# The output projection's last block of columns and the LayerNorm behind it, in halves

## The chip, the cores and the metric

The kernel runs on one core of a Trainium2 chip. The metric is the device time of one execution in microseconds, as a median of several runs. TensorE (PE) multiplies, VectorE (DVE), ScalarE (ACT) and GpSimd (POOL) work element by element, SyncE (SP) issues nearly all DMAs. Each engine works through its own queue in order and waits at semaphores for the others.

## The reference

An encoder layer over 256 tokens of 1,024 channels, all in float32. A mixer of three branches (gated linear attention, a Fourier mixing, cross-attention) ends in an output projection; its result is added to the scaled input and normalised. The normalised tokens go to a router, which picks 4 of 32 experts for each token, and to the experts:

```
h = layer_norm(DN_ALPHA * h + mix, ln1_g, ln1_b)      # mix = merged @ w_out + b_out
logits = h @ w_router + b_router                      # 1,024 x 32
top_val, top_idx = top_k(logits, 4);  top_w = softmax(top_val)
for each expert e: out = swiglu(h[tok] @ w_gu[e] + b_gu[e]) @ w_down[e] + b_down[e]
h = layer_norm(DN_ALPHA * h + weighted sum of out, ln2_g, ln2_b)
```

## The kernel before

Tokens lie in two groups of 128 partitions, tau 0 and tau 1 (`hs[tau]`, the same tiles as `h1[tau]`, 128 x 1024). In the mixer every product of the projections is made from split operands: `mm3` issues three matmuls (lines 144 to 146) of high and low parts for one step of 128 channels. A program planner orders the mixer's instructions on each engine and sets all semaphore waits from what the instructions read and write; the code sets none by hand. Within a `manual_schedule` block the order of the listed engines is that of the code.

The output projection is `project_tok(A["w_out"][0], ...)`, called twice, for columns 0 to 511 (`u == 0`) and 512 to 1023 (`u == 1`). Each call keeps two PSUM tiles of 128 x 512, one for each tau, and runs eight steps over the channels. In the first call both taus take each step in turn. In the second (`last`), all eight steps of tau 0 come first; then a written order for VectorE and TensorE begins (`K.order`, ended after `place(1)` and its picks in `moe`), tau 0 is evacuated, tau 1 has its 24 matmuls, and tau 1 is evacuated.

Evacuation is `ev_o` (lines 764 to 772). It adds the PSUM tile to the residual in `hs[tau]` and takes `bn_stats` over the 512 columns. In the second call it goes on to the LayerNorm: `bn_aggr`, the reciprocal root (`Rstd`: an add on VectorE, a power on GpSimd, in `end()` three small steps on VectorE) and two passes over 1,024 columns (lines 771 and 772), the first of which doesn't need the root.

`moe` takes over on the same written order. TensorE: two filling products of the identity (`spin`, line 901), `turn(0)` (eight transposes of tau 0, four to a PSUM tile, each taking every eighth column of `h1`, with a copy by ScalarE behind each four, lines 863 and 864), more filling, `score(0)` (line 870, the router's product with `wr`, 128 x 8 x 32), six filling products, `turn(1)`, filling, four steps of `score(1)`, `place(0)`, the other four, and the choice and gather for the first two experts. A product on float32 operands shows as two matmuls in the trace. VectorE goes from tau 1's LayerNorm to `choose(0)`, `place(0)`, `choose(1)`, `place(1)`.

The experts run two at a time in 16 pairs. Their weights, in tiles of mostly 2 MB on SyncE's queue (lines 796 and 804), go through a ring of ten buffers of 16 KB a partition, six of which are filled before the mixer ends; the other four and three further tiles use memory that the mixer's tiles gave back. A buffer is filled again as soon as TensorE has used it.

`project_T` (line 334 and on) serves the other projections: it fills a PSUM tile of two blocks of 256 columns with 24 matmuls each and then evacuates it; for the queries and keys by line 449, one instruction for each block of 256 columns.

The router's weights are loaded in the middle of the mixer by line 501, among other small loads of SyncE's queue.

Of the kernel before, what the change touches and what calls it, by code (L numbers as in the profile page):

```python
# [10 lines left out]
F32 = mybir.dt.float32  # L11
# [3 lines left out]
ALU = mybir.AluOpType  # L15
# [3 lines left out]
D = 1024  # L19
# [121 lines left out]
def mm3(K, out, w, x, first, last):  # L141
    nc = K.nc
    (wh, wl), (xh, xl) = w, x
    nc.tensor.matmul(out, wh, xh, start=first, stop=False)  # L144
    nc.tensor.matmul(out, wh, xl, start=False, stop=False)  # L145
    nc.tensor.matmul(out, wl, xh, start=False, stop=last)  # L146
# [9 lines left out]
def split_w(K, w):  # L156

    m, n = w.shape[1:]
    parts = []
    for name in ("whi", "wlo"):  # L160
        t = K.wspl.tile([128, 1024], F32R, name=name, tag=name)[:, :m * n]
        parts.append(t.rearrange("p (m n) -> p m n", m=m))
    split(K, w, *parts)
    return parts
# [33 lines left out]
def mixer(ctx: ExitStack, K, A):  # L198
    tc, nc = K.tc, K.nc
# [14 lines left out]
    def late(ap, src):  # L214
        nc.sync.dma_start(ap, src)

    def load_bc(name, ap, tag):
        t = at(name, (D,), tag=tag)
        late(t, ap[None, :].broadcast_to([128, D]))
        return t  # L220

    w_in, b_in = A["w_in"][0], A["b_in"][0]
    hs = K.h1
# [24 lines left out]
    part = K.early.tile([128, 4, D], F32, name="parts", tag="ring2")  # L248
# [19 lines left out]
    with tc.manual_schedule(engines={mybir.EngineType.DVE, mybir.EngineType.PE, mybir.EngineType.Activation}):  # L268
# [9 lines left out]
        for tau, r in enumerate((r0, r1)):  # L278
            rs_[tau] = r.end()
            c = half[2]  # L280
            t = K.small.tile([128, 8], F32, name="nmr", tag="sm")[:, 0:1]
# [4 lines left out]
            c = half[0]  # L286
            V.scalar_tensor_tensor(hs[tau][:, c], xs[tau][:, c], mvs[tau][:, 0:1], g[:, c], ALU.subtract, ALU.mult)
        for tau in range(2):
            c = half[0]
            V.scalar_tensor_tensor(hs[tau][:, c], hs[tau][:, c], rs_[tau], b[:, c], ALU.mult, ALU.add)  # L290
        for tau in range(2):
            c = half[1]
# [36 lines left out]
    def project_tok(W, c0, X, evac, last=False):  # L329

        ws = []
        for h in range(2):
            w = K.wraw.tile([128, 2048], F32, name="wraw", tag="wraw").rearrange("p (k n) -> p k n", k=4)
            nc.sync.dma_start(w, W[h * 512:h * 512 + 512, c0:c0 + 512].rearrange("(k p) n -> p k n", p=128))
            ws.append(w)
        ps = [K.ps.tile([128, 512], F32, name="pj", tag="pj") for _ in range(2)]

        def run(tau, k, parts):
            hi, lo = parts
            mm3(K, ps[tau], X.at(k, slice(tau * 128, tau * 128 + 128)), (hi[:, k % 2], lo[:, k % 2]), k == 0, k == 7)  # L340
        allp = []
        for k in range(0, 8, 2):
            parts = split_w(K, ws[k // 4][:, k % 4:k % 4 + 2])
            allp.append(parts)
            for tau in range(1 if last else 2):
                for i in range(2):
                    run(tau, k + i, parts)
            bg.tick(K.TICK)
        if last:
            K.order = tc.manual_schedule(engines={mybir.EngineType.DVE, mybir.EngineType.PE})  # L350
            K.order.__enter__()
        evac(0, ps[0])
        if last:
            for k in range(8):
                run(1, k, allp[k // 2])
        evac(1, ps[1])


    ps = K.ps.tile([128, 2, S], F32, name="pj", tag="pj")
    hi, lo = wlr_parts  # L360
# [131 lines left out]
    for u in range(2):  # L492
        sl = slice(u * 512, (u + 1) * 512)
        project_tok(w_in, 1024 + u * 512, hT,
                    lambda tau, ps: nc.vector.tensor_tensor(v[tau][:, sl], ps, bv[:, sl], ALU.add))

    late(cm, A["c_mix"])
    late(K.kp[:, 128:], A["c_keep"][:, 128:])
    late(K.wr, A["w_router"][0].rearrange("(p k) e -> p k e", p=128))
    late(K.br, A["b_router"].broadcast_to([128, NE]))  # L500
    for n in range(4):
        late(K.bias[n * 32:n * 32 + 32, 0:512], A["b_gu"][0, :, n * 512:n * 512 + 512])
# [4 lines left out]
    g1, b1 = load_bc("g1", A["ln1_g"][0], tag="g"), load_bc("b1", A["ln1_b"][0], tag="g")  # L507
# [51 lines left out]

    mv = at("mv", (2, 512), tag="o")  # L560
    project_tok(A["w_mem_kv"][0], 512, mT, lambda tau, ps: nc.scalar.activation(mv[:, tau], ps, AF.Copy))
    fnT = at("fnT", tag="o")
    project_T(w_in, 3104, 4, hT, 8, ev_id(fnT, 24))
# [185 lines left out]
        project_T(A[name][0], 0, 8, X, kn, ev_y)  # L749


    st = [K.small.tile([128, 2, 6], F32, name=f"st{t}", tag="st") for t in range(2)]

    class Merged:
        @staticmethod
# [2 lines left out]
    for u in range(2):  # L758
        sl = slice(u * 512, (u + 1) * 512)

        if u == 0:
            K.early_load(4)

        def ev_o(tau, ps):
            nc.vector.tensor_tensor(hs[tau][:, sl], hs[tau][:, sl], ps, ALU.add)
            nc.vector.bn_stats(st[tau][:, u], hs[tau][:, sl])
            if u == 1:
                mv_ = K.small.tile([128, 2], F32, name="bmv", tag="mv")
                nc.vector.bn_aggr(mv_, st[tau])
                r = Rstd(K, mv_[:, 1:2], LN_EPS, 1)  # L770
                nc.vector.scalar_tensor_tensor(hs[tau], hs[tau], mv_[:, 0:1], g1, ALU.subtract, ALU.mult)
                nc.vector.scalar_tensor_tensor(hs[tau], hs[tau], r.end(), b1, ALU.mult, ALU.add)
        project_tok(A["w_out"][0], u * 512, Merged, ev_o, last=u == 1)


# [41 lines left out]
def moe(ctx, K, A):  # L817
    tc, nc = K.tc, K.nc
    h1 = K.h1
# [4 lines left out]
    ps = ctx.enter_context(tc.tile_pool(name="eps", bufs=2, space=PSUM, reuse_waits="tile"))  # L824
# [33 lines left out]
    def turn(tau):  # L858
        hrT[tau] = big.tile([128, 8, 128], F32, name="hrT", tag="xT")
        for j in range(2):  # L860
            t = yps().rearrange("p (c n) -> p c n", c=4)
            for c in range(4):
                nc.tensor.transpose(t[:, c], h1[tau][:, j * 4 + c::8], K.ident)
            nc.scalar.activation(hrT[tau][:, j * 4:j * 4 + 4], t, AF.Copy)

    def score(tau, ks):
# [37 lines left out]

    spin(2)
    turn(0)
    spin(2)
    score(0, slice(0, 8))
    spin(6)
    turn(1)  # L910
    spin(2)
    choose(0)
# [233 lines left out]
    def back(y, p, G):  # L1146
        for n in range(2):
            combine(y, G, slice(n * 512, n * 512 + 512), p == 0, (yps, mps)[n])

    with tc.manual_schedule(engines={mybir.EngineType.DVE, mybir.EngineType.PE, mybir.EngineType.Activation}):  # L1150
# [4 lines left out]
        for p in range(1, NE // 2):  # L1155
            first = []
            a0, a = a, up(p, xT, (lambda: first.append(after(0, a, P))) if p == 1 else None)
            if p == 1:
                held = first[0]
                t = K.res.tile([128, 4, D], F32, name="sum", tag="sum", bufs=1)  # L1160
# [16 lines left out]
        st = last_down(last, now[0], G, w, parts, lambda: back(y, last - 1, held[1]))  # L1177
# [117 lines left out]
def block(tc, A):  # L1295
# [4 lines left out]
    with tc.tile_pool(name="cst", bufs=1) as c, tc.tile_pool(name="small", bufs=8) as sm, \  # L1300
# [17 lines left out]
        def early_load(e):  # L1318
# [3 lines left out]
            K.slot_no += 1  # L1322
        K.early_load = early_load
        mixer(K, A)
        with tc.tile_pool(name="res", bufs=1, side="right", reuse_waits="tile") as c:
            K.wts = c.tile([128, 2, NE], F32, name="wts")
# [39 lines left out]
```

## Time and profile before

| | before |
|---|---|
| median of 3 runs | 1233.61 us (1233.05 to 1233.71) |
| profiled execution | 1233.55 us, span 1231.5 us |
| busy: TensorE, its weight loads | 1164.2 us (95%), 639.3 us (52%) |
| busy: VectorE, ScalarE, GpSimd | 381.3 us (31%), 260.0 us (21%), 47.8 us (4%) |
| DMA | 458.24 MB, mean 372 GB/s |

The span is divided by the mixer (to about 306 us), the router (to about 320 us) and the experts. Matmuls are pipelined and their ends are modelled. The granted clock is the share of TensorE's full clock: 1.00 is 2.4 GHz and 0.50 is 1.2 GHz.

### The profile page before, as it was taken

To read this page: it belongs to the slowest core of one execution; us is meant where nothing else is said; L and a number is where in the kernel's file an instruction comes from. 1 tells how busy PE (TensorE), PEld (TensorE's weight loads), DVE (VectorE), ACT (ScalarE), POOL (GpSimd) and SP (SyncE) were. 2 spreads that over 40 slices of the span, in tenths; PEclk is the share of its full clock that TensorE was granted. 3 is DMA by queue.
4 is the path that set the end of the run, shared out by engine and by line. 5 is a ranking of instruction groups with operands and counts; after the bars stand their busy time and mean duration, and the time that the engine had idled before them with its cause. 6 is when DMAs were issued, how large, how long until landed. Compare 5 with 4: busy or idle time off the path is not lost.

```text
span 1231.5 us, 14887 instructions
## 1 busy us (share of the span) xinstructions
PE 1164.2 (95%) x6413; PEld 639.3 (52%) x6413; DVE 381.3 (31%) x591; ACT 260.0 (21%) x453; POOL 47.8 (4%) x70
## 2 busy tenths in 40 slices
PE   6999999999999999999989898999898989899995
PEld 6898999998544343443334242434243424333333
DVE  7995465486211131111202030211111111111124
ACT  4775555453111010100101010201010101000010
POOL 2150000000000000000000000000000000000000
PEclk8999999999999999999999999999999999999998
DMA  8755557687999999999999999999999999999994
GB/s 284 254 195 171 193 191 245 254 310 273 384 412 411 395 430 432 428 431 430 430 432 429 431 431 431 431 429 431 431 428 434 429 429 433 429 430 431 427 422 161
DMA packets 77241, 458.24 MB, mean 372 GB/s; under 512 B 4678, under 2 KB 39184, under 8 KB 50292
## 3 DMA queue, kind: packets, MB, share of 16 engines
q1 hardware_dynamic: 76712, 456.62, 90.5%
q8 instruction: 52, 0.85, 0.3%
q10 hardware_dynamic: 332, 0.56, 0.1%
q14 instruction: 17, 0.14, 0.0%
q0 software_dynamic: 128, 0.07, 0.0%
HBM read 456.18 MB, written 1.05 MB: 371 GB/s over the span
## 4 chain that ended last, share of the span: by engine, by line
PE 62%; DMA 34%; DVE 2%; ACT 1%; issue 0%; SPq 0%; POOL 0%; DVEq 0%; ACTq 0%
DMA wexp<-in_w_down_dram 27%; PE gps L1004 16%; PE yps L1004 15%; PE pj L146 7%; PE pj L145 7%; PE pj L144 7%; DMA wexp<-in_w_gu_dram 6%; PE mps L847 5%; PE gps L1044 1%; PE gps L998 1%; DVE wlo L118 1%; PE yps L1078 1%; PE mps L1078 1%; PE yps L998 1%; DMA first<-in_ln_in_b_dram 0%; PE mps L1136 0%
## 5 line engine op out<-in xcount | busy, mean ns | idle before, releaser
L1004 PE MATMUL gps<-wexp,xT 128*64 128x512 f32 x1984 | 447.9, 599 | 36.2 <-DMA wexp<-in_w_gu_dram 36.1
L1004 PEld LDWEIGHTS gps<-wexp,xT 128*64 128x64 f32 x1984 | 144.9, 138 | 335.1 <-issue 281.1
L1004 PE MATMUL yps<-wexp,work 128*64 128x512 f32 x960 | 220.7, 596 | 4.6 <-DMA wexp<-in_w_down_dram 4.6
L809 DVE TENSOR_SCALAR sg<-gps 128x512 f32<-128x512 f32 x31 | 21.3, 688 | 459.9 <-PE gps L1004 426.6
L1004 PEld LDWEIGHTS yps<-wexp,work 128*64 128x64 f32 x960 | 69.3, 137 | 142.9 <-issue 126.5
L118 DVE TENSOR_TENSOR wlo<-wraw,whi 128x1024 fp32r<-128x1024 f32 (+2 forms) x98 | 119.4, 1227 | 61.6 <-ACT whi L117 61.0
L810 ACT ACTIVATE sg<-sg 128x512 f32<-128x512 f32 x32 | 20.2, 630 | 489.1 <-DVE sg L809 489.1
L117 ACT ACTIVATE whi<-wraw 128x1024 fp32r<-128x1024 f32 (+2 forms) x98 | 95.4, 977 | 98.0 <-PE pj L145 82.1
L144 PE MATMUL pj<-hT,whi 128*128 128x256 f32 (+1 forms) x392 | 112.5, 287 | 0.0
L145 PE MATMUL pj<-hT,whi 128*128 128x256 f32 (+1 forms) x392 | 110.6, 282 | 0.3 <-DVE hT L118 0.3
L146 PE MATMUL pj<-hT,wlo 128*128 128x256 f32 (+1 forms) x392 | 110.6, 282 | 0.0
L1051 DVE SCALAR_TENSOR_TENSOR y<-yps,sw,y 128x512 fp32r<-128x512 f32 x30 | 22.5, 751 | 244.9 <-ACT y L1050 243.6
L145 PEld LDWEIGHTS pj<-hT,whi 128*128 128x128 f32 (+1 forms) x392 | 73.7, 188 | 1.0 <-DVE hT L118 0.8
L144 PEld LDWEIGHTS pj<-hT,whi 128*128 128x128 f32 (+1 forms) x392 | 73.7, 188 | 0.9 <-ACT whi L117 0.7
L146 PEld LDWEIGHTS pj<-hT,wlo 128*128 128x128 f32 (+1 forms) x392 | 73.6, 188 | 0.2
L847 PEld LDWEIGHTS mps<-P,h 128*128 128x128 f32 x512 | 61.6, 196 | 12.7 <-issue 12.2
L847 PE MATMUL mps<-P,h 128*128 128x128 f32 x512 | 64.8, 285 | 0.4 <-DVE P L840 0.4
L938 ACT ACTIVATE xT<-mps 128x512 f32<-128x512 f32 x32 | 19.1, 598 | 176.5 <-PE mps L847 176.5
L995 POOL COPY sel<-kp 128x128 f32<-128x128 f32 x32 | 9.5, 298 | 808.2 <-PE yps L998 483.3
L1050 ACT ACTIVATE y<-yps,sw 128x512 fp32r<-128x512 f32 x30 | 20.6, 688 | 88.1 <-PE yps L1004 78.7
L1082 DVE TENSOR_TENSOR sum<-sum,yps 128x512 f32<-128x512 f32 (+1 forms) x30 | 18.8, 666 | 22.1 <-PE yps L1078 22.1
L812 DVE TENSOR_TENSOR sg<-sg 128x512 f32<-128x512 f32 x32 | 22.1, 690 | 3.2 <-ACT sg L810 1.6
(279 smaller groups left out, 1049.3 us busy)
## 6 DMA issues: line engine op xcount, KB each, us to landing
wexp<-in_w_gu_dram SPq DMA_DIRECT2D x127, 2048.0 KB, 37.4
wexp<-in_w_down_dram SPq DMA_DIRECT2D x60, 2048.0 KB, 32.1
wraw<-in_w_in_dram SPq DMA_DIRECT2D x28, 1024.0 KB, 5.5
wexp<-in_w_down_dram SPq DMA_DIRECT2D x8, 768.0 KB, 16.4
wraw<-in_w_mem_kv_dram SPq DMA_DIRECT2D x4, 1024.0 KB
wraw<-in_w_br_gla_dram SPq DMA_DIRECT2D x4, 1024.0 KB
wraw<-in_w_out_dram SPq DMA_DIRECT2D x4, 1024.0 KB, 7.5
wraw<-in_w_br_fnet_dram SPq DMA_DIRECT2D x2, 1024.0 KB
```

The lines of the kernel that those rows point to most:

```text
L117: K.nc.scalar.activation(hi, src, AF.Copy)
L118: K.nc.vector.tensor_tensor(lo, src, hi.bitcast(F32), ALU.subtract)
L144: nc.tensor.matmul(out, wh, xh, start=first, stop=False)
L145: nc.tensor.matmul(out, wh, xl, start=False, stop=False)
L146: nc.tensor.matmul(out, wl, xh, start=False, stop=last)
L809: nc.vector.tensor_scalar(g, gate, 7.0, None, ALU.min)
L812: nc.vector.tensor_tensor(g, g, s, ALU.mult)
L847: nc.tensor.matmul(t[:, c], h1[tau][:, f0 + c % 2:f0 + 256:2], P[:, tau].rearrange("p e s -> p (e s)"), start=first and c == 0, stop=last, ...
L998: nc.tensor.matmul(ac, t[r].rearrange("k e s -> k (e s)"), bias[r, c0:c0 + ac.shape[-1]], start=first, stop=not first, skip_group_check=True)
L1004: nc.tensor.matmul(acc[e * 64:e * 64 + 64], xT[:, k, e * 64:e * 64 + 64], w[e], start=first, stop=last, skip_group_check=True)
L1051: nc.vector.scalar_tensor_tensor(y[:, 1, sl], acc, w, y[:, 0, sl].bitcast(F32), ALU.mult, ALU.subtract)
L1078: nc.tensor.matmul(c, G[:, tau * 128:tau * 128 + 128], y[:, i, sl], start=i == 0, stop=i == 1)
```

## The change

Three edits. First, in the second call of the output projection, tau 1's matmuls run in two sets, eight steps for columns 0 to 255 of the PSUM tile, an evacuation of these, then eight steps for columns 256 to 511 and their evacuation. `ev_o` takes the columns as an argument; tau 1's statistics get a third group, and each tau's statistics tile is one buffer with a tag of its own. Second, each of the two LayerNorm passes is issued in halves of 512 columns, for both taus. Third, the router's transposes take 128 adjacent columns in place of every eighth, and its weights are loaded in the order that fits: rows of 32 values (128 bytes) for each partition and step, in place of eight such rows in one piece.

```diff
         evac(0, ps[0])
         if last:
-            for k in range(8):
-                run(1, k, allp[k // 2])
-        evac(1, ps[1])
+            for c in (slice(0, 256), slice(256, 512)):
+                for k in range(8):
+                    hi, lo = allp[k // 2]
+                    mm3(K, ps[1][:, c], X.at(k, slice(128, 256)), (hi[:, k % 2, c], lo[:, k % 2, c]), k == 0, k == 7)
+                evac(1, ps[1][:, c], c)
+        else:
+            evac(1, ps[1])
...
-    late(K.wr, A["w_router"][0].rearrange("(p k) e -> p k e", p=128))
+    late(K.wr, A["w_router"][0].rearrange("(k p) e -> p k e", p=128))
...
-    st = [K.small.tile([128, 2, 6], F32, name=f"st{t}", tag="st") for t in range(2)]
+    st = [K.small.tile([128, 2 + t, 6], F32, name=f"st{t}", tag=f"st{t}", bufs=1) for t in range(2)]
...
-        def ev_o(tau, ps):
-            nc.vector.tensor_tensor(hs[tau][:, sl], hs[tau][:, sl], ps, ALU.add)
-            nc.vector.bn_stats(st[tau][:, u], hs[tau][:, sl])
-            if u == 1:
+        def ev_o(tau, ps, part=slice(0, 512)):
+            c = slice(u * 512 + part.start, u * 512 + part.stop)
+            nc.vector.tensor_tensor(hs[tau][:, c], hs[tau][:, c], ps, ALU.add)
+            nc.vector.bn_stats(st[tau][:, u + part.start // 256], hs[tau][:, c])
+            if c.stop == D:
                 mv_ = K.small.tile([128, 2], F32, name="bmv", tag="mv")
                 nc.vector.bn_aggr(mv_, st[tau])
                 r = Rstd(K, mv_[:, 1:2], LN_EPS, 1)
-                nc.vector.scalar_tensor_tensor(hs[tau], hs[tau], mv_[:, 0:1], g1, ALU.subtract, ALU.mult)
-                nc.vector.scalar_tensor_tensor(hs[tau], hs[tau], r.end(), b1, ALU.mult, ALU.add)
+                halves = slice(0, 512), slice(512, D)
+                for h in halves:
+                    nc.vector.scalar_tensor_tensor(hs[tau][:, h], hs[tau][:, h], mv_[:, 0:1], g1[:, h], ALU.subtract,
+                                                   ALU.mult)
+                r = r.end()
+                for h in halves:
+                    nc.vector.scalar_tensor_tensor(hs[tau][:, h], hs[tau][:, h], r, b1[:, h], ALU.mult, ALU.add)
...
-                nc.tensor.transpose(t[:, c], h1[tau][:, j * 4 + c::8], K.ident)
+                nc.tensor.transpose(t[:, c], h1[tau][:, (j * 4 + c) * 128:(j * 4 + c + 1) * 128], K.ident)
```

## Rows read from the trace of the kernel before

**Rows 1.** The page: the chain that ended last, shares of the span by engine.

```profile
PE 62%; DMA 34%; DVE 2%; ACT 1%; issue 0%; SPq 0%; POOL 0%; DVEq 0%; ACTq 0%
```

**Rows 2.** Stages: us, each engine's busy us (instructions), granted clock, DMA share, GB/s.

```profile
322.00:324.00 2.00, 2.00 (x12) 0.65 (x10) 0.00 (x0) 0.00 (x0) 0.00 (x0) 1.00 0.09 33
...
418.00:419.00 1.00, 1.00 (x6) 0.29 (x4) 0.00 (x0) 0.00 (x0) 0.00 (x0) 1.00 0.63 246
...
700.00:900.00 200.00, 186.85 (x879) 75.17 (x876) 34.86 (x58) 20.31 (x40) 2.48 (x8) 0.97 1.01 430
```

**Rows 3.** SyncE's waits, 312 to 328 us: for whom, total us, times, longest.

```profile
SPq L796 <- PE yps L1004: 15.0, 2, 12.0
```

**Rows 4.** Timeline, 300 to 314 us: start, us, engine, line, operation [idle before].

```profile
300.07 0.39 PE L144 MATMUL pj<-whi,mg0h 128*128 128x512 f32 x1
...
303.76 0.22 DVE L69 SCALAR_TENSOR_TENSOR rst<-rsy,ve 128x1 f32<-128x1 f32 x1 [0.44 <-POOL rsy L63]
...
304.39 1.28 DVE L772 SCALAR_TENSOR_TENSOR h<-h,rsy,b 128x1024 f32<-128x1024 f32 x1
...
305.43 0.40 PE L146 MATMUL pj<-whi,mg1l 128*128 128x512 f32 x1
...
305.87 0.69 DVE L765 TENSOR_TENSOR h<-h,pj 128x512 f32<-128x512 f32 x1 [0.19 <-PE pj L146]
...
307.32 0.21 DVE L769 BATCH_NORM_AGGREGATE bmv<-st 128x2 f32<-128x12 f32 x1
...
309.21 1.58 PE L901 MATMUL gps<-kp 128*128 128x128 f32 x12
...
310.00 1.28 DVE L772 SCALAR_TENSOR_TENSOR h<-h,rsy,b 128x1024 f32<-128x1024 f32 x1
...
311.20 0.18 DVE L874 TENSOR_TENSOR lg<-gps,br 128x32 f32<-128x32 f32 x1
...
311.43 1.13 PE L863 MATMUL yps<-kp,h 128*128 128x128 f32 x8 [0.64 <-DVE lg L874]
...
312.84 1.04 PE L870 MATMUL gps<-wr,hrT 128*128 128x32 f32 x8
```

**Rows 5.** Timeline, TensorE, 276 to 278 us: two of the matmuls of 256 columns.

```profile
276.74 0.28 PE L146 MATMUL pj<-oTh,wlo 128*128 128x256 f32 x1
...
277.10 0.28 PE L146 MATMUL pj<-oTh,wlo 128*128 128x256 f32 x1
```

**Rows 6.** Groups by form, VectorE: count | busy us, mean ns | idle.

```profile
L813 DVE SCALAR_TENSOR_TENSOR work<-work,sg 128x512 f32<-128x512 f32 x32 | 22.2, 693 | 1.1
...
L1121 DVE TENSOR_TENSOR sum<-sum,mps 128x256 f32<-128x256 f32 x2 | 0.8, 421 | 2.0 <-PE mps L1120 2.0
...
L1126 DVE BATCH_NORM_STATS2 st<-sum 128x6 f32<-128x256 f32 x8 | 2.9, 414 | 0.0
```

**Rows 7.** Timeline, 23 to 29 us: line 449 and what stands ahead of it.

```profile
23.41 2.36 DVE L118 TENSOR_TENSOR wlo<-wraw,whi 128x1024 fp32r<-128x1024 f32 x2
...
27.63 0.28 PE L146 MATMUL pj<-hT,wlo 128*128 128x256 f32 x1
...
27.95 0.88 DVE L449 TENSOR_SCALAR parts<-pj,bT 128x256 f32<-128x256 f32 x2 [2.18 <-PE pj L146]
```

**Rows 8.** Timeline, TensorE: three of eight waits for experts' weights.

```profile
645.72 7.08 PE L1004 MATMUL gps<-wexp,xT 128*64 128x512 f32 x30 [2.60 <-DMA wexp<-in_w_gu_dram]
...
880.52 8.69 PE L1004 MATMUL gps<-wexp,xT 128*64 128x512 f32 x30 [2.61 <-DMA wexp<-in_w_gu_dram]
...
1105.63 8.78 PE L1004 MATMUL gps<-wexp,xT 128*64 128x512 f32 x32 [2.59 <-DMA wexp<-in_w_gu_dram]
```

**Rows 9.** Stages, as rows 2: the microsecond after the second of these.

```profile
881.00:882.00 1.00, 1.00 (x4) 0.24 (x2) 0.00 (x0) 0.00 (x0) 0.00 (x0) 0.50 1.11 475
```

**Rows 10.** Timeline, 44 to 60 us: a load of SyncE's queue and an evacuation.

```profile
44.68 0.38 SPq L334 DMA_DIRECT2D wraw<-in_w_in_dram  x1
...
59.70 0.69 DVE L495 TENSOR_TENSOR parts<-pj,bv 128x512 f32<-128x512 f32 x1
```

## The prediction

> **What bounds the kernel now.** I read the chain of waits on the page first: TensorE has 62% of it and DMA 34% [rows 1]. The table of stages shows how these two lie in time. From 700 to 900 us the DMA share is 1.01 at 430 GB/s [rows 2], so the end is reached when the expert weights have streamed in. Before that, up to about 419 us, the stream has holes: 322 to 324 us at a share of 0.09, and the last one that I can find, 418 to 419 us at 0.63 [rows 2]. The view of SyncE's waits says what ends the first: a load of w_gu waited 12.0 us for TensorE to be through with the ring buffer of the first expert tile [rows 3]. The ring is full and TensorE frees it, so a shift of TensorE's start on the experts moves the end of each hole by as much. After the last hole the stream doesn't stop, and so the end moves by the same amount. A gain or loss of a microsecond at 320 us is therefore one in the total, although 900 us of full DMA follow.
>
> The stretch that sets this start is 300 to 320 us, in the timeline. TensorE begins tau 1's 24 matmuls at 300.07 and the last begins at 305.43. VectorE runs tau 0's LayerNorm meanwhile, whose last pass lasts from 304.39 to 305.67, takes tau 1's columns at 305.87, aggregates at 307.32 and begins its last pass at 310.00. Transposes of tau 1 begin at 311.43, the first four of its router products at 312.84 [rows 4]. TensorE was ready for the transposes at about 310.55 (12 filling matmuls from 309.21 at 0.11) and stood 0.64 us. So before the change, VectorE's LayerNorm of tau 1 is what ends last here, and TensorE has some 0.9 us to spare.
>
> **The change part by part.**
>
> *The matmuls themselves.* 24 matmuls of 512 columns become 48 of 256. The old ones start every 0.233 us ((305.43 - 300.07) / 23) [rows 4]; three of 256 columns take 0.356 us (276.74 to 277.10), 0.119 each [rows 5]. 24 x 0.119 = 2.85 us a half, 5.70 for both against 5.60: 0.1 us more.
>
> *The first half's evacuation.* It looks as if VectorE could take columns 0 to 255 at 302.9 us. It can't: both halves of the evacuation stand behind the whole of evac(0) in VectorE's written order, and that holds it until 305.7. Tau 0's two passes become two times two of 512 columns. One of these takes 0.693 us [rows 6], and independent neighbours overlap by 0.08 (line 772's pass ends at 311.28, the next instruction starts at 311.20 [rows 4]), so two come to 1.31 against 1.28. The first pair's 0.03 us lie in the 0.44 us in which VectorE waits for GpSimd's power before 303.76 [rows 4]; without that cover they would be added. The add of columns 0 to 255 then starts at about 305.61 and, at 0.421 [rows 6], ends at 306.03.
>
> *The wait that the change adds.* The second half writes columns 256 to 511 of the tile that this add reads. May TensorE write them before 306.03? One place shows how dependencies on a PSUM tile are kept here [rows 7]. Line 449 reads the two 256-column halves of one tile, and TensorE fills them one after the other. VectorE was free at 25.77 (23.41 + 2.36); the first half had been written some 2.85 us before the last matmul's end at 27.91, at 25.06. Still it stood 2.18 us and read the first half at 27.95, when the second had been written too. The wait is kept for the tile as a whole, not for its columns. I take the same for a write after a read: TensorE stands until the add is done. Bounds: from no wait (second half begins at 302.92) to a wait for the add (306.03 plus the 0.15 us that lay between line 772's end at 311.28 and the transposes at 311.43 [rows 4], so 306.17). I take the upper one, since it is the one that line 449's row speaks for. The bank rule of the Trainium skill (PSUM — Partial Sum Buffer, "PSUM bank collisions raise a hardware error") goes further than that row: a write and a read by two engines in one bank at once collide even at disjoint columns, and a semaphore has to keep them apart. By it the sum is the later one worked out below, with columns kept apart it would be the third rival's; no row of this trace shows a write held back behind a read.
>
> Behind the waiting matmul, everything on TensorE is queued: 24 matmuls, then the filling matmuls, tau 0's transposes and router products, and tau 1's.
>
> *What that costs.* With full clock: second half from 306.17 to 309.02, against 305.67 before: 3.35 us late. The work behind it takes the same 4.88 us (305.67 to 310.55), so TensorE reaches tau 1's transposes at 313.90. On VectorE: the last matmul ends at about 309.18, the add of columns 256 to 511 starts at 309.22, takes 0.42, its statistics 0.414 [rows 6]; with the 0.03 between dependent ones the aggregate starts at 310.12, 2.80 later than 307.32. Its last pass starts at 312.80, and its first half is done at 313.49, its second at 314.10. *Here the halved passes gain*: transposes of 128 adjacent columns need the first half alone for the first four, which are ready at 313.64, ahead of TensorE's 313.90; the other four follow at 314.34, ready at 314.25. So TensorE is now what is late, and tau 1's transposes start at 313.90 instead of 311.43: 2.47 us. From there the order is as before (transposes, filling matmuls, four products, placement), and what is behind them moves by the same 2.47.
>
> *The clock.* TensorE stands from about 303.1 to 306.17, 3.1 us. In the experts' stage it stood 2.59 to 2.69 us eight times (from 645.72 to 1105.63), and after three of these the granted clock was at 0.50, which is 1.2 GHz [rows 8, 9]. Behind two gaps of 2.60 and 2.61 us the same recorded matmuls took 7.08 us in one case and 8.69 in the other: a fall costs 1.61 us. Here the gap is longer than any of the eight, so I take a fall as likelier than not, at 1.61 us. The second half is dense work, as theirs was. Bounds: 0, and 3.2 for two such stretches. All before 313.90 is on the path, so it adds in full: 4.08 us.
>
> *The transposes' source and the router weights.* Eight transposes of every eighth column take 1.13 us, 0.14 each; the twelve filling matmuls, of the same size with adjacent columns, take 1.58, 0.13 each [rows 4]. The bounds are 0 and a gain of 0.01 a transpose, 0.08 for the eight of tau 1; I take 0. The router's weights are permuted to suit, so the products stay. Their load turns from 128 rows of 1 KB into 1,024 rows of 128 B on SyncE's queue. No row shows rows that small. Below, it costs nothing; above, as many rows of 1 KB are 1 MB, 2.4 us at 430 GB/s [rows 2]. I take 0 on the path: the next load behind it, at 44.68, brings the second half of rows for the second column block of v, while the first block is first evacuated at 59.70 [rows 10]; 15 us hide it. Without that cover it would be up to 2.4 us.
>
> *Other edits.* Separate one-buffer tiles for the statistics, and an aggregate over three groups rather than two: at most 0.03 us, on tau 1's chain on VectorE, which is no longer last. The DMAs that tau 1's matmuls release (one tile, then two of 1 MB) leave SyncE 3.3 us later. They were followed by the hole at 322 to 324 us, whose end moves by 2.5 to 4.1 us, so they finish at about 325.5 (with the slow clock 327.1) before the slot that ends it comes free at 326.2 (327.7): no second loss.
>
> Sum: 1233.55 (span 1231.5 and 2.05 around it; the median of the runs, 1233.61, is the same within 0.01%) + 2.47 + 1.61 = 1237.63, so 1237.6 us.
>
> **The rivals.**
> 1. *The wait, with the clock kept.* Five of the eight gaps speak for it, that all eight were shorter speaks against. 1233.55 + 2.47 = 1236.0 us.
> 2. *No wait: columns are kept apart.* It is not slower. It decides at 302.9 us: if the second half begins there, TensorE is done at 305.77, the add of the first half starts at 305.61 without a wait, and the aggregate is at 307.29, as before. What is left is the halved last pass: four transposes wait for its second half rather than eight for the whole, 0.44 us, and the copy of the first four is out of the way. About 0.5 us less: 1233.1 us. Line 449 speaks against it.
> 3. *The change disturbs the first 300 us.* Small rows, or another order by the planner, make TensorE stand there. It stands almost nowhere now. At the 2.4 us worked out above, on top of the forecast, 1240.0; an order that happens to suit it better could as well give some back.
>
> **How the numbers follow.** Chances: forecast 0.58, rival 1 0.20, rival 2 0.10, rival 3 0.12. About 0.2% (2.47 us) is what a measurement can tell here from no change, and rival 1 lies on that line, half on each side. Slower: 0.58 + 0.10 + 0.05 = 0.73. Same: 0.10 + 0.10 + 0.04 = 0.24. Faster: 0.03, from rival 3. The forecast's own range is 1236.9 to 1239.2, the top with a second slow stretch of 1.6 us. To hold the time 8 times in 10 it must take in rival 1, and since the wait's lower bound was none, it reaches to rival 2: 1233.0 to 1239.2 us.
>
> **What would show it.** In the profile after: TensorE idle for about 3 us between the two sets of 24 matmuls, ended by VectorE's add at line 770 or so; the second set from about 306.2; a granted clock of 0.50 for some 3 us from there; tau 1's first transposes 2.5 to 4.1 us after 311.43, back to back with the filling matmuls; the hole at 322 to 324 us moved as far and the experts' stage unchanged behind it. I am wrong if the second half follows the first without a gap, if the add is found ahead of tau 0's passes, or if the stream of weights has no hole left that takes over the shift.

## The result, and the profile after

The changed kernel took 1242.41 us (median of 6, 1241.0 to 1243.62) against 1233.66 us (1233.0 to 1234.09) for the kernel before in the same session: a ratio of 1.0071, 95% interval 1.0058 to 1.0084. The forecast was 1237.6 us with a range up to 1239.2. The direction was right, the loss was 8.75 us in place of 4.1. The profiled execution took 1241.23 us, with a span of 1239.5.

The page's chain of the kernel after has nearly the shares of [rows 1]; nothing new bounds it:

```profile
PE 62%; DMA 34%; DVE 3%; ACT 1%; issue 0%; SPq 0%; POOL 0%; DVEq 0%; ACTq 0%
```

The forecast's mechanism is there. This is the timeline after, 300 to 314 us, to be read beside [rows 4]; the columns are start, duration, engine, line, operation, and in brackets the idle time before it and what ended it.

```profile
300.04 0.69 DVE L771 TENSOR_TENSOR h<-h,pj 128x512 f32<-128x512 f32 x1 [2.52 <-PE pj L146]
...
302.04 0.92 POOL L63 TENSOR_TENSOR rsy<-ve,mh 128x1 f32<-128x1 f32 x1 [148.81 <-DVE ve L62]
...
302.60 0.27 PE L146 MATMUL pj<-whi,mg1l 128*128 128x256 f32 x1
303.13 0.21 DVE L69 SCALAR_TENSOR_TENSOR rst<-rsy,ve 128x1 f32<-128x1 f32 x1
...
303.76 1.42 DVE L783 SCALAR_TENSOR_TENSOR h<-h,rsy,b 128x512 f32<-128x512 f32 x2
305.10 0.41 DVE L771 TENSOR_TENSOR h<-h,pj 128x256 f32<-128x256 f32 x1
...
305.56 0.39 PE L144 MATMUL pj<-whi,mg0h 128*128 128x256 f32 x1 [2.69 <-DVE h L771]
...
308.75 0.42 DVE L771 TENSOR_TENSOR h<-h,pj 128x256 f32<-128x256 f32 x1 [2.78 <-PE pj L146]
...
311.96 1.42 DVE L783 SCALAR_TENSOR_TENSOR h<-h,rsy,b 128x512 f32<-128x512 f32 x2
...
312.09 1.58 PE L912 MATMUL gps<-kp 128*128 128x128 f32 x12
313.51 1.04 PE L874 MATMUL yps<-kp,h 128*128 128x128 f32 x8
```

TensorE stands 2.69 us between the two sets, until VectorE's add (line 771) has read the first half of the PSUM tile, and tau 1's transposes follow the filling matmuls back to back at 313.51. The clock did not fall in this execution: the view of stages (columns as in [rows 2]) has a granted clock of 1.00 (2.4 GHz) from 307 to 309 us.

```profile
307.00:309.00 2.00, 2.00 (x20) 2.00 (x19) 0.25 (x1) 0.00 (x0) 0.00 (x0) 1.00 0.00 0
```

What the forecast lacked stands in the experts' stage. Stages after (the columns of [rows 2]: busy us of the five engines, granted clock, DMA share, GB/s):

```profile
322.00:324.00 2.00, 2.00 (x11) 0.77 (x12) 0.00 (x0) 0.60 (x1) 0.00 (x0) 1.00 1.01 422
...
324.00:326.00 2.00, 2.00 (x12) 0.65 (x10) 0.00 (x0) 0.00 (x0) 0.00 (x0) 1.00 0.61 250
...
600.00:1150.00 550.00, 510.68 (x2427) 209.70 (x2424) 88.87 (x149) 52.73 (x107) 5.74 (x19) 0.98 1.01 428
...
700.00:900.00 200.00, 186.74 (x866) 74.78 (x864) 34.86 (x58) 19.73 (x39) 2.48 (x8) 0.97 1.01 427
```

The hole of 322 to 324 us has moved behind 324 us, as forecast. But from 700 to 900 us the same share of 1.01 now moves 427 GB/s, where [rows 2] had 430; from 600 to 1150 us it is 428, and before it was 430:

```profile
600.00:1150.00 550.00, 513.04 (x2452) 209.08 (x2450) 91.05 (x150) 54.66 (x112) 6.03 (x20) 0.98 1.01 430
```

Three durations tell the parts, from three starts in each timeline (tau 0's add of its last 512 columns, the first and the last expert matmul) and the end of the span.

| profiled execution | tau 0's add at | router: to the first expert matmul | experts: first to last expert matmul | rest |
|---|---|---|---|---|
| before | 300.27 | 19.74 | 896.96 | 14.55 |
| after | 300.04 | 21.97 | 902.80 | 14.65 |

The router takes 2.23 us more (forecast: 2.47 with the clock kept), and the experts, whose lines the change doesn't touch, 5.84 us more. In the timeline before, these are tau 0's add, the power of its LayerNorm on GpSimd, the first expert matmul and the group of 32 that has the last one:

```profile
300.27 0.69 DVE L765 TENSOR_TENSOR h<-h,pj 128x512 f32<-128x512 f32 x1 [2.52 <-PE pj L146]
...
302.26 1.46 POOL L63 TENSOR_TENSOR rsy<-ve,mh 128x1 f32<-128x1 f32 x1 [148.81 <-DVE ve L62]
...
320.01 1.51 PE L1004 MATMUL gps<-wexp,xT 128*64 128x512 f32 x6
...
1213.68 3.67 PE L1004 MATMUL gps<-wexp,aT 128*64 128x256 f32 x32
```

After, the first two are shown above (300.04 and 302.04), and these are the others:

```profile
322.01 1.51 PE L1015 MATMUL gps<-wexp,xT 128*64 128x512 f32 x6
...
1221.52 3.67 PE L1015 MATMUL gps<-wexp,aT 128*64 128x256 f32 x32
```

Two things that the change does could reach the weight stream: the statistics tiles with tags of their own take 160 bytes more of each partition, in front of all ring buffers (the first ring buffer begins at byte 17,664 in the program before, at 17,824 after), and the router's weights are 1,024 small rows. Theory 1 is the address, theory 2 the small rows, theory 3 the later start of the experts.

### The profile page after: what moved, and what is told of

Its sections match the earlier page's. It is cut to its first block, busy times and chain, and to the rows that moved or that the text cites. A ratio compares the mean times of both kernels' runs of the same rounds, so it can differ in the third digit from the quotient of the medians.

```text
span 1239.5 us, 14942 instructions
## 1 busy us (share of the span) xinstructions
PE 1167.3 (94%) x6437; PEld 644.5 (52%) x6437; DVE 381.7 (31%) x597; ACT 260.0 (21%) x453; POOL 46.4 (4%) x70
## 4 chain that ended last, share of the span: by engine, by line
PE 62%; DMA 34%; DVE 3%; ACT 1%; issue 0%; SPq 0%; POOL 0%; DVEq 0%; ACTq 0%
DMA wexp<-in_w_down_dram 24%; PE gps L1015 16%; PE yps L1015 14%; DMA wexp<-in_w_gu_dram 10%; PE pj L146 6%; PE pj L144 6%; PE pj L145 6%; PE mps L858 4%; PE gps L1055 1%; PE gps L1009 1%; DVE wlo L118 1%; PE yps L1089 1%; PE yps L1009 1%; PE mps L1089 1%; PE mps L1147 0%
```

## The experiments

Each was timed with the kernel before on the same chip; its medians there were 1233.89 (e1 to e4), 1233.43 (e5, e6, s128, s256), 1233.91 (e7 to e10) and 1233.52 us (e11 to e13).

**The statistics tiles alone.** The kernel before, with these two tags and nothing else; every engine's order is that of before.

```diff
-    st = [K.small.tile([128, 2, 6], F32, name=f"st{t}", tag="st") for t in range(2)]
+    st = [K.small.tile([128, 2 + t, 6], F32, name=f"st{t}", tag=f"st{t}", bufs=1)[:, :2] for t in range(2)]
```

> The kernel before with one edit: the two statistics tiles of the output projection's LayerNorm get tags of their own, one buffer each, of 2 and 3 groups (only 2 are used). No instruction changes. In the program as built, every tile allocated behind them, the experts' ring buffers among them, lies 160 bytes higher in each partition: the first ring buffer at 17,824 in place of 17,664, which is a multiple of 32 but no longer of 64. Theory 1 (the start addresses make the transfers of weights slower): the stream's rate falls from 430-431 to about 427-428 GB/s as in the changed kernel, and the time rises by 5 to 6 us, to about 1239. Theory 2 (the router's weight load of 1,024 small rows leaves the stream slower): no change, 1233.6. Theory 3 (the later or sparser start of the experts' stage makes it slower): no change, 1233.6.

1240.51 us, ratio 1.0056 (1.0042 to 1.0069). Router 19.73 us as before, experts 903.21. That speaks for theory 1, and most of the loss needs no changed instruction. Its stage, with the columns as above:

```profile
600.00:1150.00 550.00, 510.42 (x2429) 209.96 (x2426) 88.88 (x147) 54.66 (x112) 5.68 (x19) 0.98 1.01 428
```

**Is it the multiple of 64?** The kernel after with 32 bytes more in front (192 in all, ring at 17,856), and on top of that in two variants the parts of the change.

```diff
e2: [128, 3, 6] for both statistics tiles
e3: e2, and tau 1's first half in a PSUM tile of its own:
+                half = (K.ps.tile([128, 512], F32, name="pj", tag="pj") if c.start else ps[1])[:, 0:256]
e4: e2 without the split of the matmuls and of their evacuation
-            for c in (slice(0, 256), slice(256, 512)):
...
+            for k in range(8):
+                run(1, k, allp[k // 2])
+            evac(1, ps[1])
```

> The changed kernel with 32 bytes more in the statistics tiles (both of 3 groups), so that the ring buffers start at 17,856, a multiple of 64. No instruction changes. Theory 1: the rate returns to 430-431 GB/s, and only the shift of the experts' start is left, 2.0 to 2.3 us: 1235.9. If it is a multiple of 128 or more that is needed, it stays at 1241 to 1243. Theories 2 and 3: unchanged, 1241 to 1243.

> As e2_aligned, but tau 1's columns 256 to 511 go to a PSUM tile of their own, so that TensorE doesn't wait for the add of columns 0 to 255. If the wait on the tile is what moves the experts' start: the gap of 2.69 us between the two sets of 24 matmuls is gone, the experts start 0.4 to 0.5 us earlier than in the kernel before, 1233.1 with theory 1. If VectorE's order alone sets the start, the experts start as in e2_aligned, 1235.9. Theory 2 or 3 with the wait gone: about 1238.

> As e2_aligned, but tau 1 is multiplied and evacuated in one piece of 512 columns as before; the LayerNorm passes in halves, the transposes of adjacent columns and the router's weights in small rows stay. What the halved passes give by themselves: four transposes of tau 1 start after the first half. Experts' start 0.4 to 0.5 us earlier than before, 1233.1 with theory 1. With theory 2 (small rows): about 1238.5.

e2: 1241.05 us, 1.0062 (1.0048 to 1.0075), 427 GB/s: a multiple of 64 is not enough. e3: 1239.9, 1.0046 (1.0032 to 1.0059), and e4: 1239.06, 1.0042 (1.0028 to 1.0055), both at 427 GB/s with experts of 905.75 and 904.01 us; so theory 3 falls, since their experts begin earlier than before's. In e3's timeline the second set follows the first without a gap, and the add of the first half comes while it runs:

```profile
301.45 0.28 PE L146 MATMUL pj<-whi,mg1l 128*128 128x256 f32 x1
...
301.57 0.28 PE L144 MATMUL pj<-whi,mg0h 128*128 128x256 f32 x1
...
303.94 0.41 DVE L772 TENSOR_TENSOR h<-h,pj 128x256 f32<-128x256 f32 x1
```

That shows the wait to be one for the PSUM tile. Without it the router takes 19.03 us, 0.71 less than before; with one evacuation and only the halved passes and adjacent transposes 18.91, 0.83 less. In e2, which has the wait, it takes 21.96: the wait by itself is worth 2.9 us, and the rest of the change gives 0.7 of them back.

**128 and 256 bytes, and the small rows.** The kernel before with statistics tiles that take 128 or 256 bytes; and e3 at 256.

```diff
s128: [128, 2, 6], tag=f"st{t}", bufs=1       s256: [128, 5, 6], tag=f"st{t}", bufs=1
e5:   e3 with [128, 5, 6] for both
```

> The kernel before with the two statistics tiles in tags of their own, 64 bytes each: all behind them lies 128 bytes higher, the first ring buffer at 17,792, a multiple of 128 but not of 256. No instruction changes. With 160 bytes it was 6.6 us slower, and the changed kernel with 192 bytes was slow as well. If multiples of 128 are enough: 1233.9. If multiples of 256 are needed: about 1240. If any move from the old place is slow: about 1240.

> The same with statistics tiles of 128 bytes each: all lies 256 bytes higher, the first ring buffer at 17,920, a multiple of 512. If multiples of 128 or 256 are enough: 1233.9. If the finer the alignment the better: below 1233.9, by up to as much as the others lost. If any move from the old place is slow: about 1240.

> The version with tau 1's second half in a PSUM tile of its own, statistics tiles of 128 bytes each: 256 bytes higher than in the kernel before. In the run at 192 bytes its experts started 2 us earlier than in the kernel before. With multiples of 256 enough: 1233.9 less 2 = 1232. If any move is slow: about 1239.

s128: 1239.89 us, 1.0051 (1.0037 to 1.0065). s256: 1234.32, 1.0007 (0.9998 to 1.0017). The stage of s128:

```profile
600.00:1150.00 550.00, 512.87 (x2418) 210.99 (x2416) 88.08 (x147) 51.82 (x105) 5.68 (x19) 0.97 1.01 428
```

The same stage of s256:

```profile
600.00:1150.00 550.00, 511.02 (x2446) 212.09 (x2444) 91.03 (x150) 54.66 (x112) 5.97 (x20) 0.98 1.01 430
```

e5: 1233.13 us, 0.9996 (0.9987 to 1.0005), 430 GB/s. It keeps the small rows, so theory 2 falls. It was expected at 1232, from experts that began 2 us earlier in e3 than before; but 1.4 of these 2 us were a shorter mixer in that one execution (tau 0's add at 298.89 in place of 300.27), and only 0.7 are the change's. Shifts of 128, 160 and 192 bytes are slow, 0 and 256 fast.

**The change at the old addresses.** The kernel after with the statistics tiles in a pool behind the ring (which moved some tiles of the mixer by 160 bytes), and the same with 12 identity products in the gap.

```diff
e6: -    st = [K.small.tile([128, 2 + t, 6], ...
    +    st = [one.tile([128, 2 + t, 6], ...
e7: e6, and ahead of the second set:
+                for _ in range(12 if c.start else 0):
+                    nc.tensor.matmul(fill, K.ident, K.ident, start=True, stop=True)
```

> The changed kernel with its two statistics tiles in a pool of the mixer that lies behind the place of the experts' ring buffers. The instructions and their order are those of the changed kernel; the ring buffers are back at the addresses of the kernel before (the first at 17,664). Theory 1 (addresses set the stream's rate): 430-431 GB/s, only the later start of the experts is left, 2.0 to 2.3 us: 1236.0. Theory 2 (the small rows of the router's weights) and theory 3 (the later start itself slows the stream), which the first four runs already speak against: 1241 to 1243.

> The kernel after with the statistics tiles moved behind the ring (ring buffers at the kernel before's addresses), plus 12 identity products on TensorE between tau 1's two sets of 24 matmuls, so that TensorE works in the gap. If the 4.1 us of the same kernel without them are the wait for the add (2.2) and the clock's fall behind the gap (1.9): no stretch at a granted clock of 0.50 near 306 to 310 us, experts' start about 2.2 us later than before, 1233.4 + 2.2 = 1235.7 us. If the clock falls all the same, or the loss has another cause: experts' start 4.1 us later and 1237.5 to 1240 us.

e6: 1240.24 us, 1.0056 (1.0043 to 1.007); 430 GB/s again, router 23.84 us, 4.10 more than before, with the clock fallen. e7: 1237.95, 1.0036 (1.0022 to 1.005), router 22.34, clock 1.00. Both medians lie above the router's loss, by 2.7 and 1.4 us. The profiled executions show 1.9 and 1.6 us more in the mixer (first projection matmul to tau 0's add) than before's, the place where tiles had moved, but one execution each doesn't settle it, and what these microseconds are stays open. So the test was made again without moving anything in the mixer against anything else:

```diff
e11: the kernel after with [128, 5, 6][:, :2 + t] for the statistics tiles (ring at 17,920: 256 bytes further)
e12: e11 with the 12 identity products of e7
```

> The kernel after, all its edits, with two larger statistics tiles, so that everything behind them lies 256 bytes further than in the kernel before rather than 160. If the forecast's sum was right but for the address: a rate of 430 GB/s at 600 to 1150 us, experts' start 2.2 us later than before (4.1 where the clock falls behind the gap), 1235.8 to 1237.7 us. If the 6 us lie in the edits themselves: 427 to 428 GB/s and 1241 to 1242 us.

> The same with 12 identity products on TensorE between tau 1's two sets of 24 matmuls. If the wait alone is left: no granted clock of 0.50 near 306 to 310 us, experts' start 2.2 to 2.6 us later than before, 1236.0 us. The difference to the kernel without them is what the clock's fall costs, 1.5 to 1.9 us where it falls, nothing where it doesn't.

e11: 1236.91 us, 1.0027 (1.0018 to 1.0036). e12: 1235.5, 1.0018 (1.0009 to 1.0027). Both stream at 430 to 431 GB/s, with experts of 897.11 and 896.87 us. The stage of e11:

```profile
600.00:1150.00 550.00, 514.78 (x2444) 206.61 (x2440) 89.55 (x148) 54.66 (x112) 5.68 (x19) 0.98 1.01 430
```

In e11 the clock fell behind the gap; its timeline:

```profile
305.46 0.39 PE L144 MATMUL pj<-whi,mg0h 128*128 128x256 f32 x1 [2.69 <-DVE h L771]
...
308.09 0.41 PE L144 MATMUL pj<-whi,mg1h 128*128 128x256 f32 x1
...
310.12 0.42 DVE L771 TENSOR_TENSOR h<-h,pj 128x256 f32<-128x256 f32 x1 [4.26 <-PE pj L146]
...
323.38 1.94 PE L1015 MATMUL gps<-wexp,xT 128*64 128x512 f32 x8
```

Its stage there, with the granted clock third from the end (0.50 is 1.2 GHz):

```profile
307.00:309.00 2.00, 2.00 (x12) 2.00 (x11) 0.00 (x0) 0.00 (x0) 0.00 (x0) 0.50 0.00 0
```

In e12 the filling matmuls bridge the gap, and the clock holds. The timeline:

```profile
302.92 2.84 PE L358 MATMUL fill<-kp 128*128 128x128 f32 x24
...
305.76 0.38 PE L144 MATMUL pj<-whi,mg0h 128*128 128x256 f32 x1
...
322.20 1.08 PE L1018 MATMUL gps<-wexp,xT 128*64 128x512 f32 x4
```

Its stages:

```profile
307.00:308.00 1.00, 1.00 (x10) 1.00 (x10) 0.00 (x0) 0.00 (x0) 0.00 (x0) 1.00 0.00 0
...
600.00:1150.00 550.00, 514.92 (x2442) 210.16 (x2442) 90.13 (x149) 54.64 (x112) 5.68 (x19) 0.97 1.01 431
```

The router takes 23.44 us in e11 and 21.95 in e12. The change without a fall of the clock thus costs 2.21 us (the wait less what the halves give back), the fall 1.49, in sum 3.70 where the forecast had 4.08. In e6 the fall cost more, 1.87 us (23.84 against 21.97 in the kernel after). Its gap and its stage:

```profile
306.74 0.54 PE L144 MATMUL pj<-whi,mg0h 128*128 128x256 f32 x1 [2.69 <-DVE h L771]
```

```profile
307.00:309.00 2.00, 2.00 (x10) 2.00 (x10) 0.14 (x1) 0.00 (x0) 0.00 (x0) 0.50 0.00 0
```

By the trace's record of the granted clock, 0.50 lasted 3.41 us in both, from 0.07 us behind the gap in e6 and from 0.92 us behind it in e11.

**What a shifted buffer does.** The kernel before with 128 unused bytes behind a chosen ring buffer, so that only some buffers are off a multiple of 256; every engine's order is that of before. The ring is used in the order 0 to 9.

```diff
-            w = early.tile([128, 2, 2 * D], F32, name="wexp", tag=f"ring{e}")
+            w = early.tile([128, 4 * D + 32 * (e == 5)], F32, name="wexp", tag=f"ring{e}")[:, :4 * D].rearrange(...)
e9:  this; 128 off are buffers 1, 6, 7, 8, 9
e10: this and s128's tiles; 128 off are buffers 0, 2, 3, 4, 5
e13: s128's tiles, the 128 bytes behind buffer 6; 128 off are buffers 0 to 6
```

> The kernel before with 128 unused bytes between the fifth and the sixth of the ten ring buffers: five stay on multiples of 256, five lie 128 off. If each transfer pays for its own target: half of the 6 us, a rate of about 429 GB/s at 600 to 1150 us, 1236.4 us. If what counts is something else that moved with the ring's start (a table, the tiles in front of the ring, the first buffer): 1233.4 us. If one shifted buffer slows the whole queue: 1239.5 us.

> The complement: the ring starts 128 bytes later, and another 128 unused bytes lie between the fifth and the sixth buffer, so that the first five are 128 off and the last five on multiples of 256 again. If each transfer pays for its own target: again half of the 6 us, 1236.4 us. If the start of the ring is what counts: 1239.5 us, as with all ten shifted by 128.

> The kernel before with ring buffers 0 to 6 (in the order of use) 128 bytes off and 7, 8 and 9 on multiples of 256. If slow packets build up over consecutive shifted transfers, as the packets of the two half-shifted kernels look (none in the first two of a run of four, a third in the third): five of each ten transfers have slow packets, about half of the 7 us, 1237 us, and the packets over 612 ns lie in the third to seventh of each run. If the whole ring must be shifted: 1233.5 us. If seven in ten are enough for all of it: 1240 us.

e9: 1232.92 us, 0.9994 (0.9985 to 1.0003). e10: 1232.72, 0.9991 (0.9982 to 1.0). Both were expected at 1236.4: an equal cost for each shifted transfer is refuted. So is every cause in the tiles ahead of the ring, since e10 has those of s128, and in the tiles behind it, since e9 has these 128 bytes off as s128 does. The stage of e10:

```profile
600.00:1150.00 550.00, 516.07 (x2448) 210.00 (x2446) 90.91 (x150) 54.64 (x112) 6.03 (x20) 0.97 1.01 430
```

The packet records say why. A packet of 16 KB on SyncE's queue, one row of a weight tile, takes 611 ns in the kernel before, 16,993 of 17,023 of them between 500 and 1150 us (those over 640 ns, about one in 630, left out here and below). Worked out from these records, with 128 packets of the queue to a transfer and the transfers given to buffers in the program's order, the share of packets over 612 ns by ring buffer, with the shifted ones in brackets:

```
buffer      0      1      2      3      4      5      6      7      8      9    all
e9        .09  [.03]    .04    .00    .00    .00  [.01]  [.02]  [.07]  [.41]    .07
e10     [.01]    .00  [.00]  [.03]  [.11]  [.43]    .09    .00    .00    .00    .07
e13     [.01]  [.02]  [.34]  [.66]  [.59]  [.60]  [.57]    .11    .00    .00    .30
s128      all ten shifted: .60 to .67 in each                                   .64
before    none: .00 in each
```

Slow packets do not come with the first shifted transfers of a run. A run of four has most of them in its fourth, the run of seven has them from its third on, at about 0.6 from the fourth, and they run out in the next aligned transfer. (Rows of neighbouring transfers overlap in time, so a part of a share can belong to the column beside it.) The stream's rate follows the share: 430.5 GB/s before, 430.1 at .07 (e9, e10), 429.1 at .30 (e13) and 427.6 at .64 (s128), from the same records, 600 to 1150 us. e13 was expected at 1237 us, with slow packets in the third to seventh buffer, and took 1236.92, 1.0029 (1.0017 to 1.004), with 429 GB/s and experts of 900.06 us. Its stage:

```profile
600.00:1150.00 550.00, 517.09 (x2438) 218.18 (x2434) 89.52 (x148) 54.66 (x112) 5.68 (x19) 0.97 1.01 429
```

**The part that gains.** e4 with 256 bytes in place of 192 in front.

> The kernel after without the split of the matmuls and of their evacuation (halved passes, adjacent transposes and small router rows stay), with the ring buffers 256 bytes further than before. By the theory that only multiples of 256 keep the stream's rate: 430 GB/s at 600 to 1150 us, experts' start 0.8 us earlier as in the same kernel at +192, 1233.4 - 0.8 = 1232.6 us. If what slowed the stream lies in these edits and not in the address: 427 to 428 GB/s and 1238 to 1239 us.

1232.01 us, 0.9991 (0.9982 to 1.0001), 430 GB/s, router 18.90 us, experts 896.90. In its timeline tau 1's transposes (line 872) begin before the last pass has ended at 309.97:

```profile
308.56 1.41 DVE L781 SCALAR_TENSOR_TENSOR h<-h,rsy,b 128x512 f32<-128x512 f32 x2
309.60 1.15 PE L872 MATMUL yps<-kp,h 128*128 128x128 f32 x8
```

It is the lowest of all that were run. Its interval reaches 1.0001, so a version that beats the kernel before is not shown; the trace's 0.84 us are 0.07%.

## Why the prediction was wrong

- **The failed step** is "Separate one-buffer tiles for the statistics, and an aggregate over three groups rather than two: at most 0.03 us, on tau 1's chain on VectorE". As work on VectorE that was right. As memory it was 160 bytes in front of every ring buffer, and cost 6.6 us by itself (1240.51 - 1233.89 in e1). I priced what the tiles' instructions do and not where the tiles stand. "The experts' stage unchanged behind it" failed with it: 430 became 427 GB/s.
- Without that term's effect (e11), 1236.91 us were measured against the forecast's 1237.6, just at the lower edge of its own range of 1236.9 to 1239.2. Of the 0.7 us between, 0.4 are the sizes of the wait and of the clock's fall (4.08 - 3.70).
- **The wait**: right in kind, shown by e3, which takes it away by a second tile. 2.47 forecast, 2.21 to 2.23 measured. The difference is in VectorE: the forecast kept the 0.44 us of waiting for GpSimd's power ahead of 303.76 in [rows 4]. They are gone, and the root's first step runs at 303.13, since the power takes 0.92 us (302.04 in the timeline after) where it took 1.46 (302.26 in the timeline before). The rule of the Trainium skill that stood beside it (PSUM — Partial Sum Buffer, "PSUM bank collisions raise a hardware error": a read and a write in one bank must be kept apart) gave the same side, and the trace agrees: the write came 2.69 us late, when the reader was through. The planner's semaphore held it back; what the chip does without one, no run shows. Where the prediction says that columns kept apart would be the third rival's, its rival 2 is meant.
- **The clock**: a fall was called likelier than not, at 1.61 us. Its reason, a gap of 3.1 us that is longer than the eight of [rows 8], did not come true: the gap was 2.69 us, as long as the longest of them. The clock fell in e6 and e11 and not in the profiled executions of the kernel after and of e2, all with 2.68 to 2.69 us of idle time; 1.49 and 1.87 us measured. The six runs of the kernel after lie in two groups, 1241.0 to 1241.6 and 1243.2 to 1243.6. A fall in the slower three is not shown: their mean granted clock, 0.984 to 0.987, is not below the others' 0.982 to 0.983. The cause of the two groups stays open.
- **Rival 2**'s second part, about 0.5 us less without the wait, showed at 0.71 to 0.84 us where the wait was taken away (e3, e4, e5, e8). The part that it lacked is again the wait for GpSimd: in e8 the last pass begins 3.72 us behind tau 1's add (308.56 - 304.84), before 4.13 us (310.00 - 305.87).
- **Rival 3**, the small router rows at up to 2.4 us: no sign of it in e5, 1233.13 us.
- The sum for the kernel after: 2.2 (wait) and 6.6 (address) are 8.8, against 8.75 measured. That it fits so closely is luck: e2, with the same two costs (at 192 bytes), lost 7.16 us (1241.05 - 1233.89).

## What to carry to other kernels

When a stage runs at the DMA's full rate, compare the addresses of its target buffers before and after a change, even one that only adds a tag or a small tile to a pool in front: here rows of 16 KB cost 6.6 us in 1,234 when none of the ten buffers began on a multiple of 256 bytes, and nothing that the times show when half of them did. Under this planner two halves of one PSUM tile are one thing to wait for; if a matmul is to run while the other half is read, give it a tile of its own. To find out what a many-part edit does, cut its timeline at a few instructions that both kernels have, and time each piece.

## What was not expected of the hardware

- A stream of 16 KB rows into buffers that begin 128, 160 or 192 bytes past a multiple of 256 is slower by 0.7% (427.5 GB/s against 430.5), and the amount hardly depends on which: the packets' mean on SyncE's queue is 615.3 ns at 128 (s128), 615.3 to 615.4 at 160 (after, e1), 615.5 at 192 (e2 to e4), against 611.7 to 611.8 aligned.
- The cost builds up: the first two shifted transfers of 2 MB in a run have next to no slow packets, a run of four has 0.4 of them slow in its fourth, a run of seven 0.6 from its fourth on, and half the ring shifted left the time unchanged within the noise. At 430 GB/s two transfers are some 10 us. It looks as if something takes up the excess for about that long; what it is, no run shows.
- The Trainium skill has a rule that would count the excess (DMA: Bandwidth & Descriptors, "How a descriptor splits into AXI transactions"): transactions of 256 bytes begin on 256-byte addresses, and a descriptor that begins elsewhere takes one more, partly unused. For a row of 16 KB I work out from it, as an estimate, 516, 517 and 518 beats at 128, 160 and 192 bytes in place of 512: 0.8 to 1.2%. The page tells it of reads; here it is the written side that was moved, and the packets' mean grew by 0.6%, without the rule's growth from 128 to 192. That 0 and 256 bytes are fast and the three between slow agrees with the rule, the size only about; and the rule by itself doesn't say why the first shifted transfers of a run cost nothing.
- GpSimd's power in the LayerNorm takes 1.45 to 1.46 us beside a VectorE pass of 1,024 columns (before, e1, e9, e10, e13, s128, s256) and 0.92 to 0.93 beside two of 512 (the kernel after and the other experiments). Why, no run shows.
- After the same idle time of 2.68 to 2.69 us on TensorE, the granted clock stayed at 1.00 in two kernels' profiles (after, e2) and fell to 0.50 for 3.4 us in two others' (e6, e11).
